# A fused encoder layer: the first weight sum of each gate group on VectorE, the second in buffers outside the ring, and other places for the last sums in DRAM

## The chip, the cores and the metric

One core of one Trainium2 chip runs the whole layer in one launch. The metric is the device time of an execution in microseconds. The profiler's span goes from the first to the last instruction.

## The reference

One layer on 512 frames of width 1024, float32. A combined projection of the normalised input feeds three branches: gated linear attention (GLA), forgetting attention (FoX) and attention over 256 memory tokens. Each branch goes through an output weight of 512 x 1024, the results are merged by sigmoid gates, and an output projection and a squared-ReLU MLP follow.

```python
u = rmsnorm(h, g_mix[l])
proj = u @ w_in[l]                      # 1024 x 6680; the last 3 x 1024 columns are the gates
...
gt = jax.nn.sigmoid(gates.reshape(B, S, N_BRANCH, D))
merged = gt[:, :, 0] * y_gla + gt[:, :, 1] * y_fox + gt[:, :, 2] * y_mem
h = h + merged @ w_out[l]
u2 = rmsnorm(h, g_ffn[l])
h = h + jnp.square(jax.nn.relu(u2 @ w_ff1[l])) @ w_ff2[l]
```

## The kernel before

**Split arithmetic.** Each float32 operand is split into a high half (a cast on ScalarE, `whi` or `hi`) and a low half (the operand less its high half, on VectorE, `wlo` or `lo`). A product is three matmuls, high by high, low by high and high by low (lines 155 to 157). `split_w` splits one weight tile of 128 x 1024 (512 KB) into buffers from a ring of three pairs (pool `weights`, tags `hi` and `lo`); a new split waits until TensorE has finished with the pair it takes over. `load_w` loads such a tile over SP's queue.

**Seven products in place of eight.** Part of the weights goes through a scheme with seven block products (Strassen's, in Winograd's form): the weight is cut into four blocks 11, 12, 21, 22, and some products take sums of blocks: product 5 takes 11 + 12, product 6 takes 11 + 12 + 22, product 4 takes 11 + 12 + 22 + 21 (with signs carried elsewhere), product 7 takes 12 + 22. This is used for the memory and GLA gates and for the MLP's first weight.

**The gate groups.** `gate_group` runs four times: two groups for the memory gate, two for the GLA gate. They are called g0 to g3 here. A group loads block 11 into `total` and block 12 into `other` (tiles `wb`) over SP's queue, one group ahead or earlier. It then runs products 1, 2, 5, 3, 6, 7, 4 and four output tiles (`output`, whose weights come two tiles at a time through `get_o`). Between the products `total` is raised by the next block by `plus`, an accumulating DMA from DRAM on GpSimd's queue (line 935). `plus` can start when the split that read the earlier value is done. The tiles `ct` take the products; `merge` multiplies them with the output tiles on VectorE (line 991) and adds them to `acc` on GpSimd (line 992). g0 is special (`ready`): its first two weights are split before the group starts, its products come in another order, and its 11 + 12 is already made on VectorE by `vec` (line 944).

**Sums in DRAM.** The MLP's first weight needs such sums too: 32 operations (`sum_ops`) that copy or accumulate block tiles in DRAM (tiles `T`, 1 MB each from the second quarter on), also DMAs on GpSimd's queue (lines 130 and 132). `next_sum` paces them: `split_w` calls it after each cast; it counts the calls and at certain counts issues the next of the 32, which waits for that cast. Each operation that reads an earlier one's result also waits for that. The last six of them, for the last quarter, come after count 43.

**Order.** TensorE's order is the program's order. On the other engines a planner orders instructions by when it thinks them ready, and by program order among those; `tc.issue_after` holds some of them back. Each engine and each DMA queue then runs its list in order.

Of the kernel before, what the change touches and what calls it, by code (L numbers as in the profile page):

```python
# [64 lines left out]
def hybrid_block(ctx, tc, chunks, wst, memT, xN, cols, gffn, gfin, wup, cst, out):  # L65
# [6 lines left out]
    def nm(s):  # L72
        uid[0] += 1
        return f"{s}_{uid[0]}"
# [16 lines left out]
    def f(ap):  # L91
        return ap.bitcast(F32)
# [19 lines left out]
    def sum_ops():  # L112
        for q in range(4):
            for n, src, add in ((1, "11", 0), (3, "12", 0), (1, "12", 1), (3, "22", 1), (2, 1, 0), (2, "22", 1), (4, 2, 0),
                                (4, "21", 1)):
                i = index["F", q, 0 if q else 1, src] if isinstance(src, str) else None
                yield tsum[n, q], tsum[src, q] if i is None else wst[i:i + (2 if q else 1)], add

    sums = sum_ops()
    chunk_n, cast_now, low_now = [0], [None], [None]  # L120

    def next_sum(after):

        chunk_n[0] += 1
        n = chunk_n[0]
        op = next(sums, None) if (n > 23 or n > 11 and n % 2 == 0) and (n < 44 or n > 51 and n % 3 == 0) else None
        if op is not None:
            to, src, add_ = op
            if add_:
                d = nc.gpsimd.dma_start(to, src, accum_op=ALU.add, max_dma_last_dim=8192)  # L130
            else:
                d = nc.gpsimd.dma_start(to, src)
            tc.add_manual_dep(d.ins, after.name, mybir.DependencyInfo(mybir.DependencyClass.Sync, mybir.DependencyReason.DATA),
                              reason="pace")
# [7 lines left out]
    def split_w(raw):  # L142
        hi = wp.tile([P, 1024], F32R, tag="hi", name=nm("whi"))
        lo = wp.tile([P, 1024], F32R, tag="lo", name=nm("wlo"))
        cast = nc.scalar.copy(hi, raw)  # L145
        low_now[0] = nc.vector.tensor_tensor(lo, raw, f(hi), op=ALU.subtract).ins  # L146
        cast_now[0] = cast.ins
        next_sum(cast.ins)
        return hi, lo
# [57 lines left out]
    def split(hi, lo, src):  # L207
        nc.scalar.copy(hi, src)  # L208
        return nc.vector.tensor_tensor(lo, src, f(hi), op=ALU.subtract).ins  # L209
# [416 lines left out]
    def get_o(wo, j):  # L626
        return [t.rearrange("p (j k c) -> p j k c", j=2, k=4) for t in get_w(("O", wo, j // 2))]
# [94 lines left out]
    with pool("gla") as lp:  # L722
# [132 lines left out]
        ready = []  # L855
# [18 lines left out]
    def h_tile(t, name):  # L874
        return hp.tile([P, D], F32, tag=f"h{t}", name=nm(name))
# [18 lines left out]
    with pool("outp") as op_:  # L894
        def own_tile(i, g):
            return op_.tile([P, 1024], F32R, tag=f"f{i}{g}", name=nm(f"f{i}{g}"))
# [10 lines left out]
        def lefts_1():  # L907
            cast = nc.scalar.copy(S1[0], xsum[1]).ins
            nc.vector.tensor_tensor(S1[1], xsum[1], f(S1[0]), op=ALU.subtract)
            with tc.issue_after(cast):  # L910
                split(*S3, xsum[3])
# [11 lines left out]
        def gate_group(gate, wo, oh, ol, i, ready=None, last=None):  # L923
            src = {b: wst[index["W", gate, i, b]] for b in ("11", "12", "21", "22")}
            total, other = (h_tile(2 * (i % 2) + n, "wb") for n in range(2))
# [7 lines left out]
            def plus(to, b):  # L933
                with tc.issue_after(before) if before is not None else ExitStack():
                    summed[0] = nc.gpsimd.dma_start(to, src[b], accum_op=ALU.add).ins
# [7 lines left out]
            def vec(to, x, y, op=ALU.add):  # L943
                nc.vector.tensor_tensor(to, x, y, op=op)
# [4 lines left out]
            def product(n, w):  # L949
                wh, wl = (t.rearrange("p (a k c) -> p a k c", a=2, k=4) for t in w)  # L950
                uh, ul = GATE[n]
                ps = mmt([P, 2, 256])
                for a in range(2):
                    for k in range(4):
                        mm3(ps[:, a, :], wh[:, a, k, :], wl[:, a, k, :], uh[:, k, :], ul[:, k, :], k == 0, k == 3)
                return ps

            def take(n, ps):
                if n == 1:
                    nc.scalar.copy(c21, ps)  # L960
                if n == 2:
                    vec(c11, c21, ps)
                    tanh(c11)
                if n == 5:
                    nc.scalar.copy(c22, ps)
                if n == 6:
                    vec(c21, c21, ps, ALU.subtract)
                    vec(c22, c22, c21, ALU.subtract)
                if n == 3:
                    vec(c12, c22, ps)  # L970
                    tanh(c12)
                if n == 7:
                    vec(c22, c22, ps, ALU.subtract)
                    tanh(c22)
                    vec(c21, c21, ps)
                if n == 4:
                    vec(c21, c21, ps)
                    tanh(c21)
# [22 lines left out]
            if ready is not None:  # L1001
                with tc.issue_after(first):
                    ys["w"] = get_o(wo, j + 2)
                p1 = product(1, ready[0])
                with tc.issue_after(low_now[0]), tc.issue_after(cast_now[0]):
                    lefts_1()
                    vec(total, total, other)
                    take(1, p1)
            else:
                plus(total, "12")  # L1010
            plus(other, "22")
            take(2, product(2, ready[1] if ready else split_w(block("21"))))
            if ready is None:
# [5 lines left out]
            w = split_w(total)  # L1019
# [10 lines left out]
                output(j + 3)  # L1030
                p3 = product(3, split_w(block("22")))
            with tc.issue_after(cast):
                w = split_w(total)
            take(6, product(6, w))
            plus(total, "21")
            if ready is not None:
# [11 lines left out]
            with tc.issue_after(cast):  # L1048
                w = split_w(total)
# [3 lines left out]
            merge(j + 1)  # L1053

        gate_group("gate_mem", "w_mem_o", omh, oml, 0, ready=ready)
        gate_group("gate_mem", "w_mem_o", omh, oml, 1)
        omst.close()
        mhp = late.enter_context(pool("mhl"))
        mh = mhp.tile([P, KT, S], F32R, name="mh")
        ml = mhp.tile([P, KT, S], F32R, name="ml")  # L1060
        gate_group("gate_gla", "w_gla_o", ogh, ogl, 0, last=(mh, ml))
        gate_group("gate_gla", "w_gla_o", ogh, ogl, 1, last=(mh, ml))
        hN = [h_tile(t, "h") for t in range(NT)]
# [429 lines left out]
```

## Time and profile before

| | |
|---|---|
| time, median of 3 runs | 842.2 us (841.17 to 843.76) |
| the profiled execution's own time | 842.32 us |
| its span | 840.5 us |
| TensorE busy | 822.6 us (98%) |
| VectorE busy | 612.8 us (73%) |
| ScalarE busy | 461.5 us (55%) |
| GpSimd busy | 106.5 us (13%) |
| mean granted TensorE clock | 0.996 |
| DMA on GpSimd's queue | 54.01 MB, 30.6% of 16 engines' span |
| DMA on SP's and ScalarE's main queue | 96.58 MB, 32.3% |

In the rows of the timeline the columns are start and duration in microseconds, engine, line, operation, output and inputs by tile name, shape and count; in brackets stands how long the engine had been idle before, and what it waited for. PE is TensorE, DVE is VectorE, ACT is ScalarE, POOL is GpSimd, SP is SyncE. Rows of busy time by stretch give the stretch, its length, the engine's busy time in it with the number of instructions, the granted clock, the mean busy share of the DMA engines, and GB/s.

### The profile page before, as it was taken

How to read it: one execution, taken by the hardware profiler on the slowest of the kernel's cores; microseconds unless marked ns; L12 is line 12 of the kernel's file. 1: busy time of each engine (PE TensorE's matmuls, PEld its weight loads, DVE VectorE, ACT ScalarE, POOL GpSimd, SP SyncE). 2: the span in 40 equal slices, each digit the busy share in tenths (PEclk: the TensorE clock that was granted, in tenths of full speed). 3: DMA queues.
4: the chain of work that ended last, by engine and by line, in shares of the span. 5: the costliest groups of instructions: out<-in, count | busy, mean ns of one | idle time of the engine just before them, and what ended most of it. 6: DMA issues, size and time to landing. Idle time of an engine off the chain costs nothing.

```text
span 840.5 us, 12612 instructions
## 1 busy us (share of the span) xinstructions
PE 822.6 (98%) x4841; PEld 718.5 (85%) x4841; DVE 612.8 (73%) x954; ACT 461.5 (55%) x723; POOL 106.5 (13%) x129
## 2 busy tenths in 40 slices
PE   8999999999999999999999999999999999999995
PEld 6888888888888787988989889998998899889984
DVE  5856888665556685894686757896689678877897
ACT  6765777553345232543344435875577467647754
POOL 1001000001002110131441300011001100110011
PEclk9999999999999999999999999999999999999998
DMA  9525444448779582689987522968857865895543
GB/s 320 186 100 174 153 131 148 124 150 207 219 254 246 151 255 75 152 219 270 255 212 212 175 80 76 278 175 201 247 183 167 222 230 173 187 246 196 151 86 115
DMA packets 39182, 155.61 MB, mean 185 GB/s; under 512 B 4881, under 2 KB 5841, under 8 KB 37073
## 3 DMA queue, kind: packets, MB, share of 16 engines
q1 hardware_dynamic: 28288, 96.58, 32.3%
q0 software_dynamic: 9328, 54.01, 30.6%
q10 hardware_dynamic: 1504, 4.21, 1.4%
q8 instruction: 38, 0.62, 0.3%
q14 instruction: 24, 0.19, 0.1%
HBM read 152.65 MB, written 31.49 MB: 219 GB/s over the span
## 4 chain that ended last, share of the span: by engine, by line
PE 45%; DVE 5%; DMA 3%; issue 1%; ACT 1%; POOLq 0%; POOL 0%; ACTq 0%; DVEq 0%
PE mm L157 12%; PE mm L156 12%; PE mm L155 12%; PE a L156 3%; PE a L155 3%; PE a L157 3%; DMA wb<-in_wst_dram 3%; DVE wlo L146 1%; DVE h L1163 1%; DVE lo L209 1%; DVE cl L209 0%; PE a L1110 0%; ACT whi L145 0%; DVE R L1160 0%; DVE ct L991 0%
## 5 line engine op out<-in xcount | busy, mean ns | idle before, releaser
L155 PE MATMUL mm<-uhi,whi 128*128 128x512 f32 (+1 forms) x352 | 126.3, 359 | 0.6 <-ACT whi L145 0.6
L157 PE MATMUL mm<-uhi,wlo 128*128 128x512 f32 (+1 forms) x352 | 124.0, 352 | 1.0 <-DVE wlo L146 1.0
L156 PE MATMUL mm<-ulo,whi 128*128 128x512 f32 (+1 forms) x352 | 123.6, 351 | 0.0
L146 DVE TENSOR_TENSOR wlo<-raw,whi 128x1024 fp32r<-128x1024 f32 x68 | 92.2, 1359 | 35.0 <-ACT whi L145 34.7
L145 ACT CAST whi<-raw 128x1024 fp32r<-128x1024 f32 x68 | 71.2, 1049 | 63.5 <-PE mm L156 37.9
L208 ACT CAST hi<-raw 128x1024 fp32r<-128x1024 f32 x65 | 68.2, 1050 | 47.4 <-PE mm L156 34.3
L209 DVE TENSOR_TENSOR lo<-raw,hi 128x1024 fp32r<-128x1024 f32 x65 | 79.5, 1222 | 18.7 <-ACT hi L208 18.7
L157 PEld LDWEIGHTS mm<-uhi,wlo 128*128 128x128 f32 x352 | 66.6, 189 | 10.6 <-DVE wlo L146 1.4
L155 PEld LDWEIGHTS mm<-uhi,whi 128*128 128x128 f32 x352 | 66.6, 189 | 10.0 <-issue 1.0
L156 PEld LDWEIGHTS mm<-ulo,whi 128*128 128x128 f32 x352 | 66.7, 189 | 8.0
L208 ACT CAST hi<-b 128x1024 fp32r<-128x1024 f32 x40 | 41.9, 1048 | 41.4 <-PE mm L157 26.6
L156 PE MATMUL mm<-lo,ch 128*128 128x512 f32 x160 | 62.5, 391 | 0.9 <-DVE lo L209 0.9
L157 PE MATMUL mm<-u2h,lo 128*128 128x256 f32 x224 | 63.4, 283 | 0.0
L156 PE MATMUL mm<-u2l,hi 128*128 128x256 f32 x224 | 63.4, 283 | 0.0
L155 PE MATMUL mm<-u2h,hi 128*128 128x256 f32 x224 | 63.4, 283 | 0.0
L157 PE MATMUL mm<-hi,cl 128*128 128x512 f32 x160 | 62.3, 389 | 0.0
L155 PE MATMUL mm<-hi,ch 128*128 128x512 f32 x160 | 62.2, 389 | 0.0
L209 DVE TENSOR_TENSOR lo<-b,hi 128x1024 fp32r<-128x1024 f32 x40 | 48.8, 1222 | 18.2 <-ACT hi L208 18.2
L1347 POOL DMA_DIRECT2D b<-in_wst_dram x32 | 27.4, 855 | 272.5 <-DVE lo L209 208.5
L155 PE MATMUL mm<-u2sh,hi 128*128 128x256 f32 x168 | 47.5, 283 | 0.0
L156 PE MATMUL mm<-u2sl,hi 128*128 128x256 f32 x168 | 47.5, 283 | 0.0
L157 PE MATMUL mm<-u2sh,lo 128*128 128x256 f32 x168 | 47.5, 283 | 0.0
(413 smaller groups left out, 2154.3 us busy)
## 6 DMA issues: line engine op xcount, KB each, us to landing
raw<-in_wst_dram SPq DMA_DIRECT2D x114, 512.0 KB
b<-in_wst_dram POOLq DMA_DIRECT2D x32, 512.0 KB, 5.4
raw<-T SPq DMA_DIRECT2D x28, 512.0 KB
T<-in_wst_dram POOLq DMA_DIRECT2D x12, 1024.0 KB, 9.5
b<-in_wst_dram SPq DMA_DIRECT2D x16, 512.0 KB
wb<-in_wst_dram POOLq DMA_DIRECT2D x15, 512.0 KB, 5.4
wb<-in_wst_dram SPq DMA_DIRECT2D x8, 512.0 KB
T<-in_wst_dram POOLq DMA_DIRECT2D x6, 512.0 KB, 5.0
```

Of the source, the lines that this page charges most:

```text
L145: cast = nc.scalar.copy(hi, raw)
L146: low_now[0] = nc.vector.tensor_tensor(lo, raw, f(hi), op=ALU.subtract).ins
L155: nc.tensor.matmul(ps, lh, rh, start=start, stop=False)
L156: nc.tensor.matmul(ps, lh, rl, start=False, stop=False)
L157: nc.tensor.matmul(ps, ll, rh, start=False, stop=stop)
L208: nc.scalar.copy(hi, src)
L209: return nc.vector.tensor_tensor(lo, src, f(hi), op=ALU.subtract).ins
L1163: nc.vector.tensor_tensor(to, to, x, op=op)
L1347: nc.gpsimd.dma_start(to[i], wst[index["B", q, i, x]], accum_op=ALU.add)
```

## The change

Three edits. In g1, g2 and g3 the sum 11 + 12 is made on VectorE from the two loaded tiles, in place of an accumulating DMA. In the same groups the split for product 6 goes into a pair of buffers of its own (`own_tile(3)`, unused at that time) and no longer through `split_w`, so it neither takes a ring buffer nor counts in `next_sum`. And the counts at which the last six DRAM sums are issued are others.

```diff
-        op = next(sums, None) if (n > 23 or n > 11 and n % 2 == 0) and (n < 44 or n > 51 and n % 3 == 0) else None
+        op = next(sums, None) if (n > 23 or n > 11 and n % 2 == 0) and (n < 44 or n % 8 == 2 or n > 76 and n % 2 == 0) else None
...
             else:
-                plus(total, "12")
+                vec(total, total, other)
             plus(other, "22")
...
             with tc.issue_after(cast):
-                w = split_w(total)
+                if ready is not None:
+                    w = split_w(total)
+                else:
+                    w = [own_tile(3, g) for g in "hl"]
+                    split(*w, total)
             take(6, product(6, w))
```

`split` and `own_tile` exist before the change: `split` is the same cast and subtraction without ring and count, `own_tile(i, g)` gives the tile `f0` to `f3` of the stage's own pool.

## The prediction

> **What bounds the kernel now.** I read the page first, then the busy time of TensorE per gate group, its timeline at the breaks, and from there backwards: ScalarE, GpSimd and its transfers, VectorE.
>
> ```profile
> span 840.5 us, 12612 instructions
> PE 822.6 (98%) x4841; PEld 718.5 (85%) x4841; DVE 612.8 (73%) x954; ACT 461.5 (55%) x723; POOL 106.5 (13%) x129
> ```
>
> TensorE is busy 822.6 of 840.5 us. Less work on VectorE or GpSimd is therefore worth nothing by itself; only a hole in TensorE's row can close. The diff touches the four gate groups and the stage behind them. The next rows give each group's stretch (borders: first matmul of the group to first of the next) and TensorE's busy time in it.
>
> ```profile
> 337.50:369.32 31.82, 31.36 (x218) 1.00 0.68 167
> 369.32:402.75 33.43, 31.89 (x217) 1.00 0.98 253
> 402.75:435.69 32.94, 31.63 (x217) 1.00 0.91 226
> 435.69:466.89 31.20, 31.20 (x217) 1.00 0.73 214
> ```
>
> All four groups do the same matmuls: seven products and four output tiles. The fourth (call it g3) takes 31.20 us and has no hole. Over it g0 takes 0.62, g1 2.23 and g2 1.74 us. The granted clock is 1.00 in all four, so these are waits. Here are those of g1 and g2 on TensorE:
>
> ```profile
> 372.31 0.28 PE L156 MATMUL mm<-ulo,whi 128*128 128x256 f32 x1
> 372.80 0.38 PE L157 MATMUL mm<-uhi,wlo 128*128 128x256 f32 x1 [0.21 <-DVE wlo L146]
> 394.82 0.39 PE L156 MATMUL a<-oml,whi 128*128 128x512 f32 x1
> 395.05 0.39 PE L157 MATMUL a<-omh,wlo 128*128 128x512 f32 x1
> 396.00 0.38 PE L155 MATMUL mm<-uhi,whi 128*128 128x256 f32 x1 [0.56 <-ACT whi L145]
> 397.26 0.39 PE L157 MATMUL mm<-uhi,wlo 128*128 128x256 f32 x1 [0.76 <-DVE wlo L146]
> 419.50 0.28 PE L156 MATMUL mm<-f2l,whi 128*128 128x256 f32 x1
> 419.62 0.28 PE L157 MATMUL mm<-f2h,wlo 128*128 128x256 f32 x1
> 420.45 0.39 PE L155 MATMUL mm<-f1h,whi 128*128 128x256 f32 x1 [0.55 <-ACT whi L145]
> 421.71 0.39 PE L157 MATMUL mm<-f1h,wlo 128*128 128x256 f32 x1 [0.76 <-DVE wlo L146]
> ```
>
> Matmuls start 0.12 us apart with 256 columns (419.50 to 419.62) and 0.23 with 512 (394.82 to 395.05). So a product (24) lasts 2.88 and an output tile (12) 2.74 us. g1 loses about 0.4 at 372.3 (the low half of product 2 is late) and the rest, about 1.8, at product 4. g2 loses 1.7 at product 6. Both large ones begin with a late cast:
>
> ```profile
> 373.37 1.05 ACT L145 CAST whi<-wb 128x1024 fp32r<-128x1024 f32 x1 [2.50 <-DMA wb<-in_wst_dram]
> 394.90 1.99 ACT L145 CAST whi<-wb 128x1024 fp32r<-128x1024 f32 x2 [6.96 <-DMA wb<-in_wst_dram]
> 405.83 1.06 ACT L145 CAST whi<-wb 128x1024 fp32r<-128x1024 f32 x1 [2.06 <-PE mm L157]
> 419.36 1.04 ACT L145 CAST whi<-wb 128x1024 fp32r<-128x1024 f32 x1 [7.63 <-DMA wb<-in_wst_dram]
> ```
>
> The casts at 394.90 and 419.36 waited for an accumulating transfer into the weight sum. The casts for product 5 (373.37, 405.83) also wait, but nobody pays: product 5 starts at 369.32 + 2 x 2.88 + 0.46 + 2.74 = 378.3 in g1. GpSimd's row, and five transfers with their landing times (the column behind the colon in a first line is the time to issue, then stands when; the second line is issue to landing), tell why the two came late:
>
> ```profile
> 368.62 3.04 POOL L992 TENSOR_TENSOR acc<-acc,ct 128x512 f32<-128x512 f32 x2
> 378.03 0.89 POOL L935 DMA_DIRECT2D wb<-in_wst_dram  x1
> 386.15 1.78 POOL L935 DMA_DIRECT2D wb<-in_wst_dram  x2 [6.34 <-DVE wlo L146]
> ```
> ```profile
> L130 POOL DMA_DIRECT2D T<-in_wst_dram x1: 1186/1186/1186, 378.6 to 378.6; - x1
> DMA to landing us min/median/max: 12.5/12.5/12.5
> L935 POOL DMA_DIRECT2D wb<-in_wst_dram x1: 883/883/883, 386.2 to 386.2; - x1
> DMA to landing us min/median/max: 8.7/8.7/8.7
> L130 POOL DMA_DIRECT2D T<-in_wst_dram x1: 1163/1163/1163, 403.7 to 403.7; - x1
> DMA to landing us min/median/max: 10.1/10.1/10.1
> L935 POOL DMA_DIRECT2D wb<-in_wst_dram x1: 884/884/884, 410.8 to 410.8; - x1
> DMA to landing us min/median/max: 8.5/8.5/8.5
> L935 POOL DMA_DIRECT2D wb<-in_wst_dram x1: 876/876/876, 444.7 to 444.7; - x1
> DMA to landing us min/median/max: 5.0/5.0/5.0
> ```
>
> A weight sum (wb) takes 5.0 us with nothing ahead of it (444.7) and 8.7 and 8.5 where a 1 MB sum into DRAM (T) was issued before it and had not landed. The T of 378.6 landed at 391.1, the wb behind it at 394.8, 3.7 later. The T of 403.7 landed at 413.8, the wb behind it at 419.3, 5.4 later. GpSimd's transfers are served in turn, and each of the two holes is a wb behind a T.
>
> **The change part by part, and the sum.** The reference is the profiled execution: 842.32 us with a span of 840.5, 0.12 above the median 842.2.
>
> (1) **The T sums move.** Every weight split through the ring counts up, and certain counts issue a T. Before, g1 and g2 issue three each: with product 2 (counts 54, 63), product 3 (57, 66) and the second output weights (60, 69). After, product 6 of g1 to g3 is no longer counted, so a group counts 8. Counts 50, 58, 66, 74 are the second output weights of g0 and the split for product 7 in g1, g2, g3; 78 and 80 are the second and fourth w_out chunk. Six T as before, each 1 MB on the same queue, none past SP's. In g1 the T of product 3 is gone, so the wb of 386.15 should land in about 5.2 (between 5.0 and the 5.4 from 378.03 to the cast that waited for it) instead of 8.7: at 391.4, not 394.8. Product 4 is due where output ended, 395.05 + 0.23 = 395.3, less its cast and low half. The 1.8 us go, bar 0.1 that I leave for the new order. In g2 the T of product 2 is gone: the wb of 410.8 lands at 416.0, not 419.3, and product 6 is due at 419.7. Its 1.7 us go. The sums of g1 and g2 over g3 bound this: at most 2.23 + 1.74 = 3.97, at least nothing if a T again stands before the wb.
>
> For the two T in the output projection the nearest rows are g1's 1.8 us for a weight that comes late and g3's nothing. I take nothing, as the projection is matmuls on plain loads from SP's queue, with no sum for a T to stand before, and the DMA share has fallen from 0.98 in g1 to 0.73 by g3.
>
> (2) **The first sum on VectorE.** It removes three transfers of 512 KB and three issues of 0.9 us on GpSimd, and adds three additions of 1024 columns, two SBUF inputs each. Their price stands in g0, which does this already:
>
> ```profile
> 340.99 1.22 DVE L944 TENSOR_TENSOR wb<-wb,wb 128x1024 f32<-128x1024 f32 x1
> 368.15 0.68 DVE L944 TENSOR_TENSOR ct<-ct,mm 128x512 f32<-128x512 f32 x1
> 368.75 4.00 DVE L146 TENSOR_TENSOR wlo<-raw,whi 128x1024 fp32r<-128x1024 f32 x1
> 402.04 3.13 DVE L146 TENSOR_TENSOR wlo<-raw,whi 128x1024 fp32r<-128x1024 f32 x1
> ```
>
> The gain is small: product 5's cast reuses the ring buffers of product 1, whose last matmuls end at 372.2, so it moves from 373.4 to 372.4 in g1 and not at all in g2, where it already waits for TensorE. What it pushes back matters. The addition can run once product 1's low half is made and lies ahead of product 2's low half on VectorE. That one is the slow one: 4.00 us in g1 and 3.13 in g2, against 1.22 for the addition of the same shape in g0. In g1 GpSimd's merge additions run from 368.62 to 371.66, just inside the 4.00; the addition with one PSUM input at 368.15 kept its 0.68. So the new addition falls into a stretch where VectorE stands still, then product 2's low half comes 1.2 us behind it, unless the merges end earlier, as three GpSimd issues ahead of them are gone. In g1 that low half is late already. Bounds: -0.4 (g1's wait at 372.3 goes too) to 3 x 1.22 = 3.7 us. I take 0.4 kept in g1, and 0.3 and 0.4 new in g2 and g3, 1.1 in all, as the issue that leaves GpSimd (0.9) pays for most of each 1.22.
>
> [...]
>
> The addition must also precede the sum into the second buffer, which before could go out early (386.15 x2 holds g2's). GpSimd now waits for VectorE there; behind it are only merges and sums that are due later, and product 7 needs that buffer only 5 x 2.88 + 2 x 2.74 = 19.9 us into the group. Nothing.
>
> (3) **Product 6 splits into buffers of its own.** Same cast and low half; no ring buffer to wait for. Both holes waited for data, not buffers, so nothing on the path. But it leaves one more ring buffer, so the split for product 7, which now carries the T, can come an output tile (2.74 us) earlier: product 5's buffers are free before those of the output weights, which product 6 no longer leaves to it. That bears on rival one.
>
> Sum: -3.97 + 0.1 + 1.1 = -2.8, so 839.5 against 842.32; beside the median 839.4. I forecast 839.5 us, its own range 838.7 to 840.6.
>
> **Rivals.**
>
> *One, slower: a T gets ahead of a sum that is due.* In g0 count 50 lies on the second output weights, right behind the split for product 6, whose low half releases the sum for product 4.
>
> ```profile
> 353.17 1.05 ACT L145 CAST whi<-raw 128x1024 fp32r<-128x1024 f32 x1
> 353.29 1.23 DVE L146 TENSOR_TENSOR wlo<-wb,whi 128x1024 fp32r<-128x1024 f32 x1 [2.04 <-ACT whi L145]
> 354.82 1.74 POOL L935 DMA_DIRECT2D wb<-in_wst_dram  x2 [7.18 <-DVE wlo L146]
> ```
>
> The cast ends at 354.22, the low half at 354.52: a T released by the cast is ready 0.3 us before the sum. If the planner puts it first, it lands at 354.3 + 10.1 = 364.4, the sum about 4.5 later (between 3.7 and 5.4), the cast 1.05 after: 370.0. Product 4 of g0 is due at 369.32 - 2.74 - 2.88 = 363.7. That costs 6.3, so 845.8. It decides from the point where T is issued first at all. For it: the 0.3. Against: in program order the sum stands first, and before, the T of count 57 also went behind a sum (378.6 behind 378.03). The same can happen in g1 to g3 with product 7's split: a T just before the sum of 386.15 lands at 396.2, the sum at 400.7, cast and restart 401.8, product 4 due at 395.3: 6.5 us in g1 alone, so 846 and more. [...]
>
> *Two: VectorE takes it back.* Additions cost nearly 1.2 in g1 and g2 and 0.6 in g3: -3.97 + 0.1 + 0.4 + 3.0 = -0.5, so 841.8. For: the 4.00 and 3.13. Against: GpSimd's issues that leave, and g3's slack, as its low half has no wait.
>
> *Three: all holes close*, 842.32 - 3.97 = 838.35. For: g3 already runs at 31.20 with all its sums by transfer and no T issued in it. Against: the slow low half of product 2, which no part of the change takes away.
>
> *Four: nothing changes*, 842.2, if another T stands before the same sums. That is the milder form of rival one: T ready while the sum for product 6 is in flight.
>
> **How the numbers follow.** 0.3% is 2.5 us, about what can be told from no change: faster is below 839.7, slower above 844.7. Forecast 0.42 (0.30 below 839.7, 0.12 same); three 0.13 (faster); two 0.13 (same); four 0.08 (same); one 0.24 (0.21 slower, 0.03 same). Together faster 0.43, same 0.36, slower 0.21. The range 838.2 to 846.0 leaves out the far end of rival one and a little below.
>
> **What would show it.** Right: g1 and g2 last about 31.6, no T issued between 355 and product 6's low half in either, the sums for product 6 and 4 land in 5.0 to 5.5 us, and TensorE's gaps at products 4 and 6 are gone. Part two shows in the low half of product 2: over 0.5 us of wait there in g2 speaks for rival two. Wrong: a T row just before a wb row on GpSimd and a wb landing of 8 us or more; g0 longer than 31.8; a new wait of casts in the output projection behind the two T.

## The result, and the profile after

The changed kernel is slower: 856.03 us, median of five runs (854.74 to 857.05), against 843.76 (841.17 to 845.47) for the kernel before beside it. The ratio is 1.0153 with a 95% interval of 1.0134 to 1.0173. The forecast was 839.5 with a range up to 846.0. The profiled execution took 855.62 us, 13.3 more than that of before.

The head of the page after (before: span 840.5, TensorE busy 822.6):

```profile
span 853.8 us, 12607 instructions
PE 828.1 (97%) x4841; PEld 723.6 (85%) x4841; DVE 610.6 (72%) x957; ACT 460.7 (54%) x723; POOL 104.9 (12%) x126
```

The same 4841 matmuls keep TensorE busy 5.5 us longer. That can't be a wait; it says that matmuls ran slower somewhere. The busy time of TensorE per gate group, g0 to g3, says where (stretch, its length, TensorE's busy time, ..., granted clock, DMA share, GB/s):

```profile
337.69:377.27 39.58, 34.45 (x217) 31.73 (x216) 29.24 (x31) 17.03 (x21) 6.11 (x6) 0.91 0.59 145
377.27:414.67 37.40, 34.29 (x218) 31.64 (x216) 20.86 (x23) 13.06 (x17) 11.31 (x9) 0.91 0.63 155
414.67:445.79 31.12, 31.12 (x218) 29.16 (x216) 20.25 (x22) 13.26 (x17) 10.12 (x8) 1.00 0.67 203
445.79:477.00 31.21, 31.21 (x218) 29.24 (x217) 21.07 (x24) 13.02 (x18) 8.41 (x7) 1.00 0.78 202
```

g0 is 7.76 us longer than before (31.82), g1 3.97 longer (33.43), g2 1.82 shorter (32.94), g3 as it was. In g0 and g1 the granted clock is 0.91 in place of 1.00 as well. With 0.19 ahead of g0, 0.78 in the output projection and 2.46 after the last computing instruction the sum is 13.3. Here are the two breaks on TensorE:

```profile
363.56 0.28 PE L157 MATMUL mm<-f2h,wlo 128*128 128x256 f32 x1
368.25 0.58 PE L155 MATMUL mm<-uhi,whi 128*128 128x256 f32 x1 [4.42 <-ACT whi L145]
369.51 0.58 PE L157 MATMUL mm<-uhi,wlo 128*128 128x256 f32 x1 [0.46 <-DVE wlo L146]
...
402.55 0.39 PE L157 MATMUL a<-omh,wlo 128*128 128x512 f32 x1
405.57 0.58 PE L155 MATMUL mm<-uhi,whi 128*128 128x256 f32 x1 [2.64 <-ACT whi L145]
406.84 0.58 PE L157 MATMUL mm<-uhi,wlo 128*128 128x256 f32 x1 [0.47 <-DVE wlo L146]
```

Both stand at product 4 and wait for its cast. Two things are to be read: the wait itself (4.42 and 2.64), and the second column behind it, 0.58 where a matmul of 256 columns had 0.38. The cast waited for the weight sum, and GpSimd's row says why the sum was late:

```profile
367.16 1.99 ACT L145 CAST whi<-wb 128x1024 fp32r<-128x1024 f32 x2 [8.12 <-DMA wb<-in_wst_dram]
404.48 1.04 ACT L145 CAST whi<-wb 128x1024 fp32r<-128x1024 f32 x1 [12.06 <-DMA wb<-in_wst_dram]
```
```profile
354.47 0.86 POOL L130 DMA_DIRECT2D T<-in_wst_dram  x1 [6.64 <-ACT whi L145]
355.02 1.23 POOL L935 DMA_DIRECT2D wb<-in_wst_dram  x1
...
391.26 0.86 POOL L130 DMA_DIRECT2D T<-in_wst_dram  x1 [6.68 <-ACT whi L145]
391.80 1.23 POOL L935 DMA_DIRECT2D wb<-in_wst_dram  x1
```

In g0 and in g1 a T row stands right before the wb row, half a microsecond apart, and the engine had been idle for 6.6 us before the T. In the kernel before, the sum of g0 stood first (354.82). The T of 354.47 landed after 8.6 us, the sum behind it after 12.0:

```profile
DMA to landing us min/median/max: 12.0/12.0/12.0
```

In stretches of 2 us, the clock that TensorE was granted behind the first break (third column from the right):

```profile
366.00:368.00 2.00, 0.00 (x0) 0.00 (x0) 0.00 (x0) 0.84 (x1) 0.00 (x0) 0.96 0.63 242
368.00:370.00 2.00, 1.28 (x4) 0.99 (x5) 1.77 (x2) 1.15 (x2) 0.00 (x0) 0.50 0.00 0
370.00:372.00 2.00, 2.00 (x11) 2.00 (x11) 1.97 (x4) 1.26 (x2) 0.00 (x0) 0.50 0.73 258
372.00:374.00 2.00, 2.00 (x12) 2.00 (x11) 1.71 (x3) 0.00 (x0) 0.81 (x1) 0.50 0.01 4
374.00:376.00 2.00, 2.00 (x10) 1.74 (x10) 1.39 (x2) 1.05 (x1) 1.73 (x2) 0.83 0.00 0
376.00:378.00 2.00, 2.00 (x14) 1.76 (x13) 1.94 (x2) 0.75 (x1) 0.65 (x1) 1.00 0.03 8
```

For 6.83 us (367.85 to 374.67) the clock is 0.50. Product 4 takes 6.13 us (368.25 to 374.38) instead of the 2.88 of a product that runs without a wait; part of the difference is the wait for the low half. The count beside TensorE's busy time shows the same: 10 to 12 matmuls in 2 us, where 18 and 19 stand in the run with the filled hole below.

The last computing instruction is the same in both kernels, but the program ends later after it: 840.5 - 836.71 = 3.79 us before, 853.8 - 847.55 = 6.25 after. The rows are those of before and after:

```profile
835.96 0.75 DVE L1290 SCALAR_TENSOR_TENSOR h<-h,rr,gl 128x512 f32<-128x512 f32 x1 [0.44 <-POOL rr L889]
```
```profile
846.80 0.75 DVE L1294 SCALAR_TENSOR_TENSOR h<-h,rr,gl 128x512 f32<-128x512 f32 x1 [0.44 <-POOL rr L889]
```

So three questions were open: is it the order of T and sum alone; do the other two edits cost something; and what are the half clock and the longer end.

### The profile page after: what moved, and what is told of

It is laid out like the page before. It is cut to its first block, busy times and chain, and to the rows that moved or that the text cites. A ratio compares the mean times of both kernels' runs of the same rounds, so it can differ in the third digit from the quotient of the medians.

```text
span 853.8 us, 12607 instructions
## 1 busy us (share of the span) xinstructions
PE 828.1 (97%) x4841; PEld 723.6 (85%) x4841; DVE 610.6 (72%) x957; ACT 460.7 (54%) x723; POOL 104.9 (12%) x126
## 5 line engine op out<-in xcount | busy, mean ns | idle before, releaser
L155 PE MATMUL mm<-uhi,whi 128*128 128x512 f32 (+1 forms) x352 | 128.6, 365 | 7.1 <-ACT whi L145 7.1
L157 PE MATMUL mm<-uhi,wlo 128*128 128x512 f32 (+1 forms) x352 | 126.3, 359 | 0.9 <-DVE wlo L146 0.9
L156 PE MATMUL mm<-ulo,whi 128*128 128x512 f32 (+1 forms) x352 | 125.7, 357 | 0.0
L146 DVE TENSOR_TENSOR wlo<-raw,whi 128x1024 fp32r<-128x1024 f32 x68 | 85.3, 1257 | 37.6 <-ACT whi L145 36.9
L155 PEld LDWEIGHTS mm<-uhi,whi 128*128 128x128 f32 x352 | 68.8, 195 | 16.7 <-ACT whi L145 7.7
L157 PEld LDWEIGHTS mm<-uhi,wlo 128*128 128x128 f32 x352 | 68.7, 195 | 10.7 <-DVE wlo L146 1.5
L156 PEld LDWEIGHTS mm<-ulo,whi 128*128 128x128 f32 x352 | 68.9, 196 | 8.0
```

What stands on the lines that cost most here:

```text
L155: nc.tensor.matmul(ps, lh, rh, start=start, stop=False)
L156: nc.tensor.matmul(ps, lh, rl, start=False, stop=False)
L157: nc.tensor.matmul(ps, ll, rh, start=False, stop=stop)
```

## The experiments

The texts call theory Q: T ahead of a due sum on GpSimd's queue sets nearly all of the loss. Its rivals are V in the first round (the additions or the own buffers cost the time) and P in the second (the additions and the order of the work in the groups do).

### First round: which edit

**The changed kernel with T one count later.**

```diff
-... (n < 44 or n % 8 == 2 or n > 76 and n % 2 == 0) else None
+... (n < 44 or n % 8 == 3 or n > 76 and n % 2 == 0) else None
```

> The changed kernel with its counts moved by one (n % 8 == 3 in place of 2), so that in g0 and g1 the T is issued behind the weight sum that is due for product 4 and not before it. Nothing else differs. Theory Q (a T issued before a due sum makes the sum late): g0 back from 39.6 to about 31.8 us, g1 from 37.4 to 31.2 to 31.8, sums for products 6 and 4 landing in 5.0 to 5.5 us, clock 1.00 in all groups, time 838 to 841. Theory V (the addition on VectorE or the buffers of product 6's own cost the time): g0 or g1 stay long, time above 850.

Measured: 847.87 us, ratio to before 1.0046 (1.0027 to 1.0066). The sum for product 4 goes first in every group and lands 5.4 to 6.5 us after its issue; g0 and g1 take 31.9 and 31.2. So the order of two rows on GpSimd is worth 8.2 us of the 12.3. But the total misses Q's 838 to 841: 4 us stay, and they stand elsewhere: waits of 0.99 and 1.05 us at the low half of product 2 in g2 and g3, 1.98 at the start of the output projection, and an end of 6.29.

**The changed kernel with the counts of before.**

```diff
-... (n < 44 or n % 8 == 2 or n > 76 and n % 2 == 0) else None
+... (n < 44 or n > 51 and n % 3 == 0) else None
```

> The changed kernel with the old counts (n > 51 and n % 3 == 0): the addition on VectorE and product 6's own buffers alone. Theory Q: g0 31.8; in g1 a T (count 57) again stands between the sums for products 6 and 4, so a late sum of 8 to 9 us there and a hole of 1 to 3 us, as before the change; time 840 to 845. Theory V: 850 or more.

Measured: 858.26, ratio 1.0177 (1.0150 to 1.0205). A miss. Counts alone say nothing: with product 6 out of the count they fall on other splits. A T of 410.00 stands before the sum of product 6 of g2 (413.67), which costs a wait of 3.42 us and a clock of 0.50 again. That is only a part of the loss: the waits at the low half of product 2 are 1.17, 1.45 and 1.07 us in g1 to g3, product 4 of g1 and g2 is late by 0.8 to 1.7, the output projection by 2.26, and the end is 6.31.

**The kernel before with the new counts.**

```diff
-... (n < 44 or n > 51 and n % 3 == 0) else None
+... (n < 44 or n % 8 == 2 or n > 76 and n % 2 == 0) else None
```

> The kernel before with the new counts alone, first sums by transfer as before. Theory Q: in g0 the T stands before the sum for product 4 and g0 takes 39 to 40 us with the half clock behind the hole; in g1 a T also stands before the sum for product 4, with a hole of 2 to 5 us; time 850 to 858. Theory V: about 842, since the additions and the buffers are as before.

Measured: 857.57, ratio 1.0162 (1.0144 to 1.0181). As Q had it: without the other two edits the loss is as large. T rows stand before the due sums of g0, g1 and g3, with waits of 4.25, 1.73 and 2.04 us, each followed by a clock of 0.50. The output projection (58.56 us from its first matmul to the first feed-forward matmul on a ring buffer, `u2h,whi`; so measured in all runs) and the end (3.80) are those of before. In this profiled execution 2.0 us stand ahead of g0, where the two kernels do the same: its clock was at 0.50 from 12.4 to 19.3 us.

**The changed kernel with all six T late.**

```diff
-... (n < 44 or n % 8 == 2 or n > 76 and n % 2 == 0) else None
+... (n < 44 or n > 76) else None
```

> The changed kernel with the last six T all behind count 76, so none in the gate groups. Theory Q: all four groups at 31.2 to 31.8 us, all weight sums land in 5.0 to 5.5 us, time 838 to 841; what g2's low half of product 2 still waits is the price of the addition on VectorE. Theory V: above 850. If the T themselves cost by bandwidth in the output projection, that stage (58.6 us before) grows by some us.

Measured: 852.61, ratio 1.0107 (1.0084 to 1.0130). A miss. The output projection takes 67.33 us, where the one-later run with two T in it takes 60.83 and before 58.56; the waits are spread over it (2.57 at its start, then 0.3 to 1.2). It does not hide six T.

### Second round: each edit on a kernel without the T

The base is the kernel before with each T right behind a due sum.

```diff
-... (n < 44 or n > 51 and n % 3 == 0) else None
+... (n < 44 or n in (51, 60, 69, 78, 81, 83)) else None
```

> The kernel before with one edit: the six T sums from count 51 on stand at counts 51, 60, 69, 78, 81 and 83, so that each goes to GpSimd's queue behind the weight sum that is due, never ahead of it. Additions on GpSimd and the ring stay as in before. Theory Q (the order of T and due sum on GpSimd's queue sets nearly all of the changed kernel's loss, and the two holes of before had the same cause): groups 0 to 3 all near 31.2 to 31.9 us, no granted clock below 0.9 inside them, last compute to end of program 3.8 us, total 838 to 841. Theory P (it is the additions and the plan of the groups that set the time, T's place only moves a hole): a hole of 1 us or more appears at another product, total 842 to 847.

Measured: 839.07, ratio 0.9945 (0.9925 to 0.9965), faster than before. Its groups:

```profile
337.57:369.46 31.89, 31.42 (x217) 29.16 (x216) 27.76 (x30) 16.93 (x21) 6.44 (x8) 1.00 0.77 178
369.46:400.59 31.13, 31.13 (x218) 29.16 (x216) 19.89 (x21) 13.08 (x17) 10.06 (x11) 1.00 0.78 201
400.59:431.71 31.12, 31.12 (x218) 29.16 (x216) 20.66 (x21) 12.81 (x16) 10.66 (x10) 1.00 0.84 234
431.71:462.83 31.12, 31.12 (x218) 29.16 (x216) 22.72 (x25) 14.61 (x20) 9.37 (x8) 1.00 0.80 210
```

The length equals the busy time in g1, g2 and g3, as the forecast wanted for the change. The places of the T alone do it; in g0 that is one count, 51 in place of the changed kernel's 50. GpSimd's row there has the sum (x2, with the next group's first sum) and then T.

```profile
354.96 1.75 POOL L935 DMA_DIRECT2D wb<-in_wst_dram  x2 [7.24 <-DVE wlo L146]
356.08 1.52 POOL L130 DMA_DIRECT2D T<-in_wst_dram  x1
```

**The addition alone, on that base.**

```diff
-                plus(total, "12")
+                vec(total, total, other)
```

> The kernel with T at counts 51, 60, 69, 78, 81, 83 and on top the addition total + other by VectorE instead of GpSimd's queue, in all four groups; the ring as in before. If the addition is what is left of the loss beside T's order (the one-later run stood 4 us above before): waits of 1.0 to 1.3 us at the low half of product 2 in at least two groups, a hole of about 2 us where the output projection starts, and 6.3 us instead of 3.8 from the last compute to the end, so 845 to 849. If the addition costs only the 1.1 us that the prediction took: 839 to 842, with the end at 3.8 us.

Measured: 840.56, ratio 0.9964 (0.9950 to 0.9977). The output projection starts at 462.70, against 462.83 on the base: inside the groups the three additions cost nothing, and no low half of product 2 is late. The end is 6.25 instead of 3.83. Neither expectation had this pair. (The edit bears on g1 to g3; in g0 the sum is on VectorE in both.)

**The own buffers alone**, with T in much the same places:

```diff
-... (n < 44 or n > 51 and n % 3 == 0) else None
+... (n < 44 or n % 8 == 3 or n > 76 and n % 2 == 0) else None
...
-                w = split_w(total)
+                if ready is not None:
+                    w = split_w(total)
+                else:
+                    w = [own_tile(3, g) for g in "hl"]
+                    split(*w, total)
```

> The kernel before with only the third edit (the split for product 6 of group 0 into buffers of its own) and the T sums at every eighth count from 51 on and even counts above 76; additions on GpSimd's queue. If the own buffers matter to nothing: the time of the run with T at 51, 60, 69, 78, 81, 83 within 1 us, 838 to 841, end of program 3.8 us. If the ring was holding product 6: group 0 shorter than 31.5 us. If T sums in the output projection cost: more than 58.6 us from the start of the output projection to the first feed-forward product, total above 842.

Measured: 845.48, ratio 1.0020 (1.0008 to 1.0033), some 6 us above the base. (The edit bears on g1 to g3; g0 goes through the ring in both.) The waits are those of the one-later run: the low half of product 2 in g2 (1.00) and g3 (0.53), and the start of the output projection (2.26 us), which takes 62.70 us. VectorE's row in g3, this run first, then the base:

```profile
449.81 1.23 DVE L209 TENSOR_TENSOR f3l<-wb,f3h 128x1024 fp32r<-128x1024 f32 x1 [4.52 <-ACT f3h L208]
450.95 1.22 DVE L146 TENSOR_TENSOR wlo<-wb,whi 128x1024 fp32r<-128x1024 f32 x1
452.19 1.23 DVE L146 TENSOR_TENSOR wlo<-raw,whi 128x1024 fp32r<-128x1024 f32 x1
458.27 1.23 DVE L146 TENSOR_TENSOR wlo<-wb,whi 128x1024 fp32r<-128x1024 f32 x1 [4.86 <-ACT whi L145]
459.41 0.68 DVE L944 TENSOR_TENSOR ct<-ct,mm 128x512 f32<-128x512 f32 x1
460.12 0.69 DVE L944 TENSOR_TENSOR ct<-ct,ct 128x512 f32<-128x512 f32 x1
```
```profile
449.86 1.23 DVE L146 TENSOR_TENSOR wlo<-raw,whi 128x1024 fp32r<-128x1024 f32 x1 [0.37 <-ACT whi L145]
451.78 0.69 DVE L944 TENSOR_TENSOR ct<-ct,mm 128x512 f32<-128x512 f32 x1 [0.69 <-PE mm L157]
452.50 0.69 DVE L944 TENSOR_TENSOR ct<-ct,ct 128x512 f32<-128x512 f32 x1
454.83 1.23 DVE L146 TENSOR_TENSOR wlo<-wb,whi 128x1024 fp32r<-128x1024 f32 x1 [1.64 <-ACT whi L145]
```

On the base the two subtractions that take product 6 (451.78, 452.50) run while the sum for product 4 is under way, and the low half of product 4 comes behind them. With the own buffers product 4's low half stands first in the list. It waits 4.86 us for the sum's cast, with the subtractions ready behind it. Everything after them on VectorE (the takes of products 3 and 7, the merges) moves back. TensorE pays at the next product 2, whose low half is made behind them, and at the output projection, which waits for a merge (line 991):

```profile
470.64 0.50 PE L155 MATMUL a<-whi,mh 128*128 128x512 f32 x1 [2.26 <-DVE ct L991]
```

### Third round: the order, the end, the clock, the queue

**The own buffers, with VectorE's list put back.**

```diff
-                    vec(c22, c22, c21, ALU.subtract)
+                    taken[0] = nc.vector.tensor_tensor(c22, c22, c21, op=ALU.subtract).ins
...
-            with tc.issue_after(cast):
+            with tc.issue_after(cast), tc.issue_after(taken[0]) if ready is None else ExitStack():
                 w = split_w(total)
             take(4, product(4, w))
```

> The run with the own buffers alone, and one edit more: the split for product 4 is held until the two subtractions that take product 6 have been issued, so that VectorE's list is that of the run with T at 51, 60, 69, 78, 81, 83, buffer names aside. Theory O (the own buffers cost time only because, with a ring pair left over, the planner puts product 4's split ahead of the takes of product 6 in VectorE's list, where it waits for the sum to land and holds the takes and merges behind it): no waits over 0.3 us at the low half of product 2, none of 2 us where the output projection starts, 58.6 us from there to the first feed-forward product, total 838 to 841. Rival (the own buffers themselves, or the two T sums in the output projection, cost it): total stays at 844 to 847 and the output projection at 62 us or more.

Measured: 838.41, ratio 0.9949 (0.9936 to 0.9961). Theory O holds: 7 us come back by the order of three rows on VectorE in each of g1 to g3, the output projection takes 58.55, and no wait of 0.3 us is left at any product 2.

```profile
451.43 0.69 DVE L944 TENSOR_TENSOR ct<-ct,mm 128x512 f32<-128x512 f32 x1 [1.86 <-PE mm L157]
452.15 0.69 DVE L968 TENSOR_TENSOR ct<-ct,ct 128x512 f32<-128x512 f32 x1
454.50 1.23 DVE L146 TENSOR_TENSOR wlo<-wb,whi 128x1024 fp32r<-128x1024 f32 x1 [1.66 <-ACT whi L145]
```

The own buffers by themselves cost nothing and give nothing.

**The end of the program.** The addition run again, with three copies of 512 KB of no use on GpSimd's queue early in the program, and with one.

```diff
+        if n in (6, 8, 10):
+            d = nc.gpsimd.dma_start(junk, wst[0:1])
...
```

The other run has `n in (8,)`.

> The run with the addition on VectorE alone, with three copies of 512 KB within DRAM of no use on GpSimd's queue near the start, so that the queue carries as many transfers as before the addition left it. If the long end of program follows the number of transfers on GpSimd's queue: 3.8 us from the last compute to the end instead of 6.3, total near 838 to 839. If it follows the addition or the order of the gate groups: 6.3 us, total 840 to 842.

> As the run with three copies, with one copy. If the end grows with each transfer that is missing: about 5.5 us. If it has two values only: 3.8 or 6.3 us.

With three copies: 839.65, ratio 0.9965 (0.9952 to 0.9978), and the end is 836.6 - 832.77 = 3.83 us. With one copy (one execution, 841.51) it is 839.7 - 833.37 = 6.33.

```profile
832.02 0.75 DVE L1294 SCALAR_TENSOR_TENSOR h<-h,rr,gl 128x512 f32<-128x512 f32 x1 [0.44 <-POOL rr L893]
```
```profile
832.62 0.75 DVE L1294 SCALAR_TENSOR_TENSOR h<-h,rr,gl 128x512 f32<-128x512 f32 x1 [0.44 <-POOL rr L893]
```

So the addition isn't itself what lengthens the end. It leaves GpSimd's queue three transfers short, and the end goes with how many that queue has carried: with 79 it is 3.79 us (before) and 3.83 (three copies), with 76 it is 6.25 (the changed kernel and the addition alone), with 77 it is 6.33 (one copy). In the traces of before and after it goes with GpSimd's last long DRAIN, an instruction near the end of its list: 4.75 us before, 7.32 in the changed kernel. Which property of the number decides was not tried.

**The clock.** The changed kernel with 36 matmuls of no use in the hole of g0.

```diff
+                for i in range(fill):
+                    nc.tensor.matmul(ps[:, i % 2, :], uhi[:, 4, 256:384], uhi[:, 4 + i % 4, 256:512], start=True, stop=True)
...
-            take(4, product(4, w))
+            take(4, product(4, w, 0 if ready is None else 36))
```

> The changed kernel with 36 matmuls of 256 columns of no use ahead of product 4 of group 0, into the PSUM tile that product 4 then overwrites: they fill the 4.6 us in which TensorE waits for the late sum, and the sum is as late as before. If the drop of the granted clock to 0.50 follows TensorE's idle time: the clock stays near 1.00 through group 0's product 4, which takes 2.9 us instead of 6.1, group 0 near 36 us instead of 39.6, total near 852.5; group 1 keeps its drop. If the drop has another cause (the DMA traffic or the hour of the program): product 4 stays at 5.5 to 6.1 us and the total at 856 or above.

Measured: 854.61, ratio 1.0127 (1.0099 to 1.0154).

```profile
366.00:368.00 2.00, 2.00 (x19) 2.00 (x19) 0.00 (x0) 0.00 (x0) 0.00 (x0) 1.00 1.04 274
368.00:370.00 2.00, 1.90 (x16) 1.68 (x14) 0.33 (x1) 1.41 (x2) 0.00 (x0) 1.00 0.40 162
370.00:372.00 2.00, 1.24 (x10) 1.05 (x9) 1.97 (x3) 1.06 (x2) 0.00 (x0) 1.00 0.10 18
372.00:374.00 2.00, 2.00 (x18) 1.96 (x17) 2.00 (x4) 0.98 (x3) 0.00 (x0) 1.00 0.66 250
```

The clock stays at 1.00, with the sum as late as in the changed kernel (12.0 us). So the drop in this hole went with TensorE's idle time: with 4.42 us of it the clock fell to 0.50, with the hole filled it did not. g0 takes 37.58 us in place of 39.58, so the half clock cost 2.0 us there, not the 3.5 expected: product 4 still waits for its low half (0.76) and takes 4.00. The total says little of it: 1.2 us more than in the changed kernel stand ahead of g0 (clock 0.50 from 11.2 to 18.0 us), and the fill also changed the planner's list for g1, where the sum now goes first (392.95, T at 393.50). g1 takes 31.1, and the loss of the one-later run appears in g2, g3 and the output projection.

**Queue or bandwidth.** The changed kernel with the T of count 50 moved one count on, and a plain copy of 1 MB on ScalarE's queue in its old place.

```diff
+        if n == 50:
+            d = nc.scalar.dma_start(junk, wst[0:2])
...
```

> The changed kernel with T's place at count 50 taken by a plain copy of 1 MB within DRAM on ScalarE's queue, and the T sum itself at count 51, behind the due sum on GpSimd's queue. Queue (a due sum is late because GpSimd's queue serves T first): the sum for product 4 in group 0 lands within 5 to 7 us of its issue, no hole there, group 0 near 32 us. Bandwidth (it is late because T's bytes take the DMA engines): it lands 9 us or more after its issue and the hole stays above 2 us. Group 1 keeps its hole in both.

One execution, 854.4 us. The sum for product 4 of g0 goes first and lands after 8.7 us:

```profile
DMA to landing us min/median/max: 8.7/8.7/8.7
```

That is between the two. With nothing beside it at its issue it took 5.5 (addition alone), behind T 12.0. So of the 6.5 us that T costs the sum, about half (3.2) also comes from 1 MB on another queue, and the other half only from standing behind T. TensorE's wait was 0.79, not 4.42. g0 still took 35.6 us and not the 32 of theory Queue, since the clock fell to 0.50 here too, from 366.26 to 369.68. The copy was a plain one, T accumulates, and it is one execution, so the split is rough.

**All three edits, both orders mended.** T one count later, and the split for product 4 held as above.

> The changed kernel with T one count later (n % 8 == 3) and the split for product 4 held until the takes of product 6 have been issued; additions on VectorE and own buffers as in the change. If the three causes are all: no hole of 1 us in the gate groups or at the start of the output projection, no granted clock below 0.9 there, 6.3 us from the last compute to the end, total 839.5 to 841.5, some 2.4 above the run with the hold on the kernel before. If the additions cost time only together with the own buffers: waits of 0.5 us or more at the low half of product 2 and a total of 842 to 846.

Measured: 841.34, ratio 0.9963 (0.9949 to 0.9976). No wait over 0.7 us is left in the groups or at the output projection (58.81), the end is 6.29. So the two orders together decide between 856.03 and 841.34; the longer end is what then remains against the base.

## Why the prediction was wrong, point by point

**What bounds the kernel**: right. TensorE's holes in the groups were the only thing to gain, and both of before were a wb behind a T. The base of the second round closes them by T's places alone and gains 0.55%, where the forecast had 842.2 to 839.4, or 0.33%.

**(1) The T sums move: the step that failed.** "In g1 the T of product 3 is gone, so the wb of 386.15 should land in about 5.2" is true of the T that was there, and the new T was taken to go behind the due sum. It went ahead, in g0 and in g1. The prediction had the rows for it: a cast that ends 0.3 us before the low half that releases the sum. It gave program order more weight than readiness. The planner orders by when it thinks an instruction ready, and by program order only among those; that stands in the text on the kernel. A T at count 50 was put ahead of the sum in all three runs that have one, a T at 51 behind it in all nine. At product 7's split in g1 (count 58) it went ahead in the changed kernel and behind in the run with the filled hole, where only the matmuls of no use were added. The 1.7 us of g2 did go (31.12), with the sum ahead of its T there.

**Rival one** is what happened, with its mechanism and places; its chance was 0.24. Its price was nearly right for half the reason: 6.3 in g0 and 6.5 in g1 were forecast, 7.76 and 37.40 - 31.20 = 6.2 measured. The data came earlier than reckoned (product 4 started at 368.25, not 370.0), and a clock of 0.50 that the prediction did not have at all added 2.0 us in g0 by the run with the filled hole; in g1 product 4 took 6.12 us as well, but no run fills that hole. So that the price came so near is in part luck. And it was priced for g0 or for g1, while the same rule in the planner holds in both: the two together lead to 856, and the range ended at 846.0.

GpSimd's transfers land in the order in which they were issued, all 79 in the trace of before and all 76 in that of the changed kernel; T's landing at 363.07 and the sum's at 367.06 are two of them. By the run with the copy on another queue (8.7 us, against 5.5 alone and 12.0 behind T; one execution), order is about half of the delay.

**(2) The addition on VectorE**: the term was 1.1, between -0.4 and 3.7. Measured inside the groups: -0.1. The longer rows are there: in the changed kernel the three additions took 1.59, 1.93 and 2.01 us (375.22, 410.23, 441.74), against 1.22 in g0, and ran wholly or in part beside GpSimd's merge additions (373.19 to 375.72, 409.80 to 413.31, 441.37 to 444.90). But VectorE's list had room, and TensorE waits for none of them: its row shows no wait at a product 2 of g1 to g3. What the edit costs, 2.4 us, stands where the prediction did not look, at the end of the program, by transfers that GpSimd no longer carries.

**(3) Own buffers: "nothing"** was the second wrong term. Data, not buffers, held both holes, as it said, and it saw that a ring pair left over lets a later split come earlier; it followed that only to product 7 and T. The split for product 4 came earlier too, ahead of the takes of product 6 on VectorE. On a kernel without T's trouble that costs 6 to 7 us. In the changed kernel the list has that order in g2 and g3 (in g3 the low half of product 4 waits 4.56 us, and the takes follow at 469.00), but only 0.78 us of it shows, at the output projection; why so little was not tried.

**The T in the output projection: nothing** holds for two (58.56 on the base); for six it does not (67.33).

**Rivals two, three and four**: none of them. VectorE's additions took nothing back in the groups. The holes of g1 and g2 do all close, but on the base of the second round and not by this change. Four had another T before the same sums at the price of before; in g1 it was the same sum, and g1 grew by 3.97 us.

## What to carry to other kernels

Where a planner orders a queue, read the list it makes, and not the program: two DMAs that become ready 0.3 us apart can come in either order, and here one order costs 6 to 8 us a group. An edit that frees a buffer or a slot moves every later instruction that was held by it; look for one that now stands at the head of an engine's list and waits for a transfer (here product 4's low half, 4.86 us, with two subtractions ready behind it). And a hole on TensorE can cost more than its length: behind those of 4.42 and 2.64 us in the changed kernel the matmuls ran at a clock of 0.50 for up to 6.83 us, which in g0 was 2.0 us of time.

## What the runs showed of the hardware

**The granted clock after a hole.** In the traces of before and of the changed kernel it is 1.00 or 0.50 at any moment (other values are means over a stretch). In the changed kernel it changes at 367.85, 374.67, 405.39, 412.22 and, behind the last matmul, 845.71. These lie 6.83, 30.72, 6.83 and 433.49 us apart, which are 2, 9, 2 and 127 steps of 3.41. In the run with the copy on another queue it falls at 366.26, 403.81 and 478.91, which are 11 and 22 such steps apart.

Half clock lasted 6.83 us behind the waits of 4.42 and 2.64 in the changed kernel. In the run with the copy it lasted 3.4 us each time: behind waits of 0.79 and 0.76, of 3.32 and 0.76, and of 2.16. It also lasted 3.4 behind the wait of 2.26 with the own buffers alone. What decides between the two lengths is open.

In the changed kernel the two steps ahead of the drops held 3.41 and 2.46 us of TensorE's idle time. No other step at full clock up to 830 us held more than 1.10, or 0.97 in the kernel before, and none of those was followed by half clock. In the run with the copy the step up to 366.26, with waits of 0.79 and 0.76, was followed by it. The length of a wait alone doesn't tell: waits of 2.57 (all six T late), 2.49 (the filled hole, at the output projection) and 1.98 (T one count later) left the clock at 1.00, while one of 1.73 with 0.76 behind it (new counts alone) was followed by matmuls 0.21 us apart in place of 0.12. What else decides is open.

**The last long drain of GpSimd** takes 4.75 us in the trace of before, with 79 transfers on its queue, and 7.32 in that of the changed kernel, with 76. The program's end behind the last computing instruction, 3.79 and 6.25 us, follows it. Why is open.
